# The second product of a gated MLP as seven block products, with its operands and weights in a ring of 512-column tiles

## The chip, the cores and the metric

One core of a Trainium2 chip. The metric is the device time of one execution in microseconds (us), the median of the runs shown. About half a per cent is what a measurement of this kernel can tell from no change.

## The reference, cut to what matters

One inference step of a hybrid decoder layer on 512 prompt tokens and 64 sample tokens (8 sequences of 8): sparse attention, a gated linear recurrence, a merge, and a gated MLP with a causal depthwise convolution of width 3. The change concerns the last lines, the MLP.

```python
def merge_and_ffn(x, o_a, o_b, ma, mb, w_branch, w_out, ffn_norm_g, ffn_w_in, ffn_conv_w, ffn_conv_b, ffn_w_out, conv_buf):
    m = ma * (o_a.astype(x.dtype) @ w_branch[:A_WIDTH]) + mb * (o_b @ w_branch[A_WIDTH:])
    x = x + m @ w_out
    h = rms_norm(x, ffn_norm_g)
    a, b = jnp.split(h @ ffn_w_in, 2, axis=-1)
    ...
    a_conv = ffn_conv_b + sum(a_ext[:, j:j + T] * ffn_conv_w[j] for j in range(FFN_CONV))
    y = x + (jax.nn.silu(a_conv) * b) @ ffn_w_out
```

The model width is 1024 (8 tiles of 128), the hidden width 2816 (22 tiles of 128), and all tensors are fp32.

## The kernel before

Data lie transposed: 128 features on the partitions, the 576 tokens along the free dimension, in two halves of HF = 288 columns. A product in fp32 accuracy is made of three products of a format that TensorE takes at full rate (fp32r): each operand is split into a high part and the rest (`split`, L326: a cast on ScalarE, L330, then a subtraction, L331, on VectorE, or on GpSimd for one split in `pool_every`), and `THREE` multiplies high by high, high by rest and rest by high. `wsplit` (L341) loads a weight tile into `wraw` and splits it into `wsp`; `gemm` (L360) runs, for each contraction tile, the three products on both token halves, 288 columns a matmul.

The kernel runs as one unrolled program in which a scheduler at build time sets each engine's order of instructions; every engine then works through its own queue in that order and waits on semaphores. Stages in order of time: the recurrence, the projections, prompt and sample attention (to about 646 us), `merge` (L1739), `out_proj` (L1783) and `ffn` (L1823). From `merge` on, weights live in the pool `ringF` (L436) with three `wraw` tiles of 1024 columns and three `wsp` tiles of twice 1024, and products in four PSUM tiles `ps_g` of two banks.

`ffn` has two loops. The first (L1834) makes the 22 hidden tiles: for each, one weight tile, 48 matmuls (L1841), an eviction with the norm's factor (L1844 to L1846, VectorE from PSUM), the convolution (L1851 to L1853, VectorE), Silu (L1855 to L1858, ScalarE), a product on GpSimd (L1859), a second weight tile, 48 matmuls (L1861), the gate (L1863) and a split into `g` (L1865), which holds all 22 tiles. The second loop (L1867) makes the 8 output tiles: for each, the residual row `x2r` is loaded (L1869), three weight tiles (8, 8 and 6 blocks, L1874) are multiplied with all of `g`, 132 matmuls into one PSUM tile, one addition on VectorE (L1877) and one store (L1879).

## Time and profile before

| | us |
|---|---|
| median of 3 runs | 1143.64 |
| lowest and highest | 1141.67, 1147.85 |
| the profiled execution, its time | 1141.99 |
| the profiled execution, its span from first to last instruction | 1140.2 |

Times in the rows are those of the profiled execution, counted from its first instruction; 1.8 us of its time lie outside the span. PE is TensorE, PEld its weight loads (which run beside its matmuls), DVE VectorE, ACT ScalarE, POOL GpSimd, SP the queue that issues most DMAs. In a row of groups, `out<-in` names the tiles written and read; behind the first bar stand the busy time and the mean duration of one instruction in ns, behind the second the idle time of that engine just before them and what ended it. A duration includes time that an instruction, once started, is held up.

### The profile page before, as it was taken

Reading aid. Unit: us, or ns where it says so; the run is one execution under the profiler, and the core shown is the slowest. Engines: PE = TensorE matmul, PEld = TensorE weight load, DVE = VectorE, ACT = ScalarE, POOL = GpSimd, SP = SyncE. Lnnn points to the kernel's source line nnn. Section 1 sums busy time; section 2 is a strip of 40 time slices with the busy share of each in tenths; the row PEclk is TensorE's granted clock in tenths of the full one; section 3 lists DMA queues with packets and bytes.
Section 4 is the critical chain, followed back from the end, with each engine's and each line's share of the span. In section 5 each row is a group of like instructions: output and inputs, shape, how many; then the busy total and the mean of one; then the engine's idle time right before and its main releaser. Section 6 shows DMA issues by size and latency. Waiting matters only on the chain.

```text
span 1140.2 us, 21336 instructions
## 1 busy us (share of the span) xinstructions
PE 1092.3 (96%) x7936; PEld 1034.8 (91%) x7936; DVE 658.1 (58%) x1182; ACT 470.8 (41%) x929; POOL 430.4 (38%) x514
## 2 busy tenths in 40 slices
PE   5999999999999899999888799999999999999998
PEld 5997999898999899899665699999999999999998
DVE  6768555674257756887776664665555555511110
ACT  5523443443444567776565643332223222311110
POOL 3654513833374535343365354232223222301010
PEclk8999899999999999999899999999999999999999
DMA  5634456454342422273789675322232223334330
GB/s 199 185 103 155 126 160 194 131 156 149 124 148 59 131 88 72 77 224 101 222 274 284 208 220 183 93 91 88 79 93 75 85 83 93 99 104 124 102 115 21
DMA packets 99273, 151.54 MB, mean 133 GB/s; under 512 B 11233, under 2 KB 66274, under 8 KB 99042
## 3 DMA queue, kind: packets, MB, share of 16 engines
q1 hardware_dynamic: 97714, 146.00, 41.2%
q0 software_dynamic: 1024, 3.54, 1.0%
q8 instruction: 62, 1.02, 0.4%
q10 hardware_dynamic: 432, 0.65, 0.2%
q14 instruction: 41, 0.34, 0.1%
HBM read 131.65 MB, written 22.62 MB: 135 GB/s over the span
## 4 chain that ended last, share of the span: by engine, by line
PE 60%; DVE 6%; ACT 2%; DMA 1%; issue 1%; POOL 1%; SPq 0%; DVEq 0%; ACTq 0%; POOLq 0%
PE ps_g L367 44%; PE ps_g L1200 2%; PE ps_hp L1307 2%; PE ps_sb L1299 2%; PE ps_po L1634 1%; DVE r L1138 1%; PE ps_sa L1267 1%; PE ps_g L1763 1%; PE ps_g L1773 1%; POOL rr L1128 1%; PE ps_sm L1333 1%; PE ps_g L1333 1%; DMA nraw<-in_wk 1%; PE ps_sa L1260 0%; PE ps_sc L1551 0%
## 5 line engine op out<-in xcount | busy, mean ns | idle before, releaser
L367 PE MATMUL ps_g<-h,wsp 128*128 128x288 f32 x2112 | 279.8, 294 | 0.0
L367 PEld LDWEIGHTS ps_g<-h,wsp 128*128 128x128 f32 x2112 | 279.4, 188 | 0.1
L330 ACT CAST wsp<-wraw 128x1024 fp32r<-128x1024 f32 (+3 forms) x142 | 136.3, 966 | 281.0 <-PE ps_g L367 240.5
L367 PE MATMUL ps_g<-xg,wsp 128*128 128x288 f32 x1200 | 182.9, 305 | 16.4 <-ACT wsp L330 8.8
L367 PEld LDWEIGHTS ps_g<-xg,wsp 128*128 128x128 f32 x1200 | 167.7, 193 | 23.6 <-ACT wsp L330 9.0
L331 DVE TENSOR_TENSOR wsp<-wraw,wsp 128x1024 fp32r<-128x1024 f32 (+2 forms) x93 | 113.5, 1222 | 116.4 <-ACT wsp L330 116.1
L331 POOL TENSOR_TENSOR wsp<-wraw,wsp 128x1024 fp32r<-128x1024 f32 (+3 forms) x49 | 108.0, 2203 | 187.1 <-ACT wsp L330 183.7
L367 PE MATMUL ps_g<-g,wsp 128*128 128x288 f32 x1056 | 140.9, 296 | 0.0
L367 PEld LDWEIGHTS ps_g<-g,wsp 128*128 128x128 f32 x1056 | 140.8, 189 | 0.0
L528 PE MATMUL ps_t<-wsp,xg 128*128 128x262 f32 (+1 forms) x480 | 60.9, 285 | 0.0
L528 PEld LDWEIGHTS ps_t<-wsp,xg 128*128 128x128 f32 x480 | 58.9, 189 | 0.1
L903 PE MATMUL ps_pc<-phi,w 128*128 128x256 f32 x256 | 51.0, 290 | 0.0
L330 ACT CAST phi<-praw 128x2048 fp32r<-128x2048 f32 x16 | 30.4, 1901 | 45.7 <-PE ps_pc L903 27.6
L1848 POOL COPY cout<-ext 128x2 f32<-128x2 f32 x22 | 4.1, 184 | 119.0 <-DVE ext L1845 119.0
L1155 POOL TENSOR_TENSOR zg<-zg,rsb 128x576 f32<-128x576 f32 x16 | 27.2, 1699 | 56.4 <-ACT zg L1154 56.4
L1863 DVE TENSOR_TENSOR s<-ps_g,s 128x576 f32<-128x576 f32 x22 | 16.6, 757 | 51.5 <-POOL s L1859 51.5
L1855 ACT ACTIVATE s<-cv 128x512 f32<-128x512 f32 x22 | 13.9, 632 | 78.6 <-DVE cv L1853 78.6
L331 DVE TENSOR_TENSOR plo<-praw,phi 128x2048 fp32r<-128x2048 f32 x14 | 32.7, 2338 | 22.4 <-ACT phi L330 22.2
L903 PEld LDWEIGHTS ps_pc<-phi,w 128*128 128x128 f32 x256 | 42.1, 196 | 0.8 <-issue 0.8
L1274 ACT ACTIVATE sP<-sP,nm 128x128 f32<-128x128 f32 (+3 forms) x64 | 35.6, 560 | 9.2 <-DVE nm L1272 9.2
L1844 DVE TENSOR_TENSOR ext<-ps_g,rs 128x288 f32<-128x288 f32 x22 | 10.1, 457 | 50.8 <-PE ps_g L367 50.7
L1859 POOL TENSOR_TENSOR s<-s,rs 128x576 f32<-128x576 f32 x22 | 31.6, 1434 | 18.8 <-ACT s L1858 18.8
(428 smaller groups left out, 1983.0 us busy)
## 6 DMA issues: line engine op xcount, KB each, us to landing
wraw<-in_wFi SPq DMA_DIRECT2D x44, 512.0 KB
praw<-in_pc SPq DMA_DIRECT2D x256, 64.0 KB
praw<-in_pkv SPq DMA_DIRECT2D x80, 128.0 KB
wraw<-in_wM SPq DMA_DIRECT2D x16, 512.0 KB
wraw<-in_wFo SPq DMA_DIRECT2D x16, 512.0 KB
gbd<-zg SPq DMA_DIRECT2D x24, 288.0 KB
wraw<-in_wBr SPq DMA_DIRECT2D x24, 256.0 KB
pgs<-in_pkv SPq DMA_DIRECT2D x48, 128.0 KB
```

The source lines that it names most:

```text
L330: self.copied = nc.scalar.copy(hi, src)
L331: (eng or nc.vector).tensor_tensor(lo, src, hi.bitcast(F32), op=ALU.subtract)
L367: self.last = nc.tensor.matmul(ps[:, h, 0:HF], w[:, cw, wk, :], (x[cx] if isinstance(x, list) else x[:, cx])[:, xk, h * HF:(h + 1) * HF], ...
L528: nc.tensor.matmul(ps[:, 0:n], self.xg[cx][:, k, j * 128:j * 128 + 128], w[k][:, cw], start=(k == 0 and c == 0), stop=(k == KT - 1 and c = ...
L903: self.nc.tensor.matmul(ps, self.w1[:, cw, j, k], x[cx][:, k], start=start and k == 0 and n == 0, stop=k == 7 and n == 2, skip_group_check ...
L1155: nc.gpsimd.tensor_tensor(z, z, self.rsb, op=ALU.mult)
L1200: self.last = nc.tensor.matmul(ps, w[:, cw, k], self.obs[cx][:, k, c], start=n == 0, stop=n == 11)
L1274: nc.scalar.activation(s[:, b], s[:, b], AF.Exp, scale=-1.0, bias=nm[:, 1 + b, i:i + 1], accum_out=sm[:, 1 + b, i:i + 1])
L1299: nc.tensor.transpose(ps[:, n * 128:n * 128 + 128], sP[i][:, b, j * 128:j * 128 + 128], self.cst("ident"))
L1307: last = nc.tensor.matmul(po[:, i * 128:512], vs[:, j, b].rearrange("p a d -> p (a d)"), pt[:, c, n * 128:(n + m) * 128], start=first, sto ...
L1333: self.last = nc.tensor.matmul(ps, w[:, cw, k], self.oas0[:, cx, k], start=n == 0, stop=n == 11)
L1859: nc.gpsimd.tensor_tensor(s, s, self.rs2, op=ALU.mult)
```

## The change

In `ffn`, the 22 hidden tiles are taken as 11 pairs. For a pair of hidden tiles, a pair of output tiles and the two token halves, the product is one of 2 by 2 blocks, and it is computed with seven block products in place of eight (Winograd's form of Strassen's scheme), each still three matmuls of 288 columns.

- `moving` makes, for each pair of hidden tiles, the seven moving operands: four as they stand or negated, three sums on GpSimd (on VectorE in part for the last pair), all split into high part and rest.
- `down_weights` makes, for a pair of output tiles `q` and a chunk of `m` pairs of hidden tiles, the seven stationary operands: two loads, four sums (three on VectorE, one on GpSimd), seven splits (of the subtractions two on GpSimd).
- The hidden width is taken in chunks of 3, 4 and 4 pairs. After the hidden tile that follows a chunk, `down` runs the chunk's products for the four pairs of output tiles, adds the results to what the earlier chunks left (at first `x2d`) and stores it to a buffer in DRAM, `y2d`; the last chunk stores to `yT`. Within `down`, seven products go to four PSUM banks; two banks receive a second product after the first has been read. The last product of each `q` is issued within the next one. In the last chunk the first four products begin with three of the four pairs.
- From `merge` on, all split weights lie in a ring of ten tiles `w4` of twice 512 columns (before: three `wsp` of twice 1024), and the raw weights in four tiles in place of three. A 1024-column weight tile is split in two halves (`whalves`). The order of the weights in DRAM is changed to match.
- The body of the first loop is moved to a function, `hidden`, and is as before but for the two halves and for the split of its result, which `moving` does for a pair.

```diff
-    a["wFo"] = ktiles(ffn_w_out[0], 128)
+
+    wo = ffn_w_out[0].reshape(NF // 2, 2, 128, 4, 2, 128)
+    a["wFo"] = c(wo.transpose(3, 1, 2, 4, 0, 5)[:, ::-1])
...
+CHUNKS = (3, 4, 4)
+NW4 = 10
...
+    def whalf(self, src, eng=None):
+        sp = self.ring.tile([128, 2, 4, 128], F32R, name="w4", tag="w4", bufs=NW4)[:, :, 0:src.shape[1]]
+        self.split(sp[:, 0], sp[:, 1], src, eng=eng)
+        return sp
...
+    def whalves(self, dram):
+        raw = self.wload(dram, KT, 128)
+        out = []
+        for i in range(2):
+            self.nsplit += 1
+            out.append(self.whalf(raw[:, 4 * i:4 * i + 4], self.nc.gpsimd if self.nsplit % self.pool_every == 0 else self.nc.vector))
+        return out
...
+            self.nraw = 4
...
-        w = self.wsplit(self.a["wO"][d], KT, 128)
+        w = self.whalves(self.a["wO"][d])
...
-                    w = self.wsplit(a["wO"][d], KT, 128)
+                    w = self.whalves(a["wO"][d])
...
+    def moving(self, p, X, Y, last):
+        nc = self.nc
+        e = V if last else G
+        H = lambda y, x: Y[:, y, x * HF:x * HF + HF]
+        ts = p.tile([128, 4, HF], F32, name="ts", tag="ts", bufs=1)
+        flat = Y.rearrange("p a t -> p (a t)")
+        self.split(X[:, 0, 0:2], X[:, 1, 0:2], Y[:, :, 0:HF])
+        G.tensor_tensor(ts[:, 0:2], Y[:, :, HF:T], flat[:, 0:T].rearrange("p (a t) -> p a t", a=2), op=ALU.subtract)
+        e.tensor_tensor(ts[:, 2], ts[:, 0], H(1, 1), op=ALU.subtract)
+        e.tensor_tensor(ts[:, 3], ts[:, 2], H(1, 0), op=ALU.add)
+        self.split(X[:, 0, 3:7], X[:, 1, 3:7], ts)
+        self.split(X[:, 0, 2], X[:, 1, 2], H(1, 1), scale=-1.0)
...
+    def down_weights(self, q, c0, m, early=False):
...
+        fl = lambda t: t[:, :, 0:m]
+        dram = self.a["wFo"][q]
+        raw = []
+        for i in (1, 0):
+            t = self.ring.tile([128, 2, 4, 128], F32, name="wraw", tag="wraw", bufs=self.nraw)
+            nc.sync.dma_start(fl(t), dram[i][:, :, c0:c0 + m])
+            raw.append(fl(t))
+        (a, c), (b, d) = ((t[:, 0], t[:, 1]) for t in raw)
+        s13, s24 = (fl(self.ring.tile([128, 2, 4, 128], F32, name="wsum", tag="wsum", bufs=2)) for _ in range(2))
...
+        w["a"] = self.whalf(a)
+        V.tensor_tensor(s13[:, 0], c, d, op=ALU.add)
+        V.tensor_tensor(s24[:, 0], s13[:, 0], a, op=ALU.add)
+        w["s2"] = self.whalf(s24[:, 0])
+        w["s1"] = self.whalf(s13[:, 0])
+        V.tensor_tensor(s13[:, 1], c, a, op=ALU.add)
+        G.tensor_tensor(s24[:, 1], s24[:, 0], b, op=ALU.add)
+        if early:
+            w["d"] = self.whalf(d)
+        w["s3"] = self.whalf(s13[:, 1])
+        w["b"] = self.whalf(b, G)
+        if not early:
+            w["d"] = self.whalf(d, G)
+        w["s4"] = self.whalf(s24[:, 1])
+        return w
...
+    def down(self, p, n, c0, g, nxt):
...
+        m = len(g)
+        end = c0 + m == NF // 2
...
+        def product(ps, w, x, first, js=range(m)):
+            for j in js:
+                for cw, cx in THREE:
+                    self.last = nc.tensor.matmul(ps, w[:, cw, j], g[j][:, cx, x], start=first and j == 0 and (cw, cx) == (0, 0),
+                                                 stop=j == m - 1 and (cw, cx) == THREE[2], skip_group_check=True)
...
+        def finish(q, w, pc, vv, za, zb, y):
+            product(pc, w["s4"], 2, False)
+            V.tensor_tensor(za[:, HF:T], vv, pc, op=ALU.subtract)
+            for i, z in enumerate((za, zb)):
+                nc.sync.dma_start(self.o["yT"][:, 2 * q + i] if end else self.y2d[n, 2 * q + i], z)
...
+        rest = None
+        A, B, begun = self.bank("g"), self.bank("g"), ()
+        if end:
+            for ps, x, i in ((A[:, 0], "a", 0), (A[:, 1], "s2", 5), (B[:, 0], "s1", 3), (B[:, 1], "d", 6)):
+                product(ps[:, 0:HF], nxt[x], i, True, range(m - 1))
+            begun = (0,)
+        for q in range(4):
+            w = nxt
+            za, zb = (p.tile([128, T], F32, name="z2", tag=t) for t in ("ext", "cv"))
+            src = self.y2d[n - 1] if n else self.x2d
+            nc.sync.dma_start(za, src[2 * q])
+            nc.sync.dma_start(zb, src[2 * q + 1])
+            if q:
+                A, B = self.bank("g"), self.bank("g")
+            pa, pb, pc, pd = (t[:, h, 0:HF] for t in (A, B) for h in range(2))
+            js = range(m - 1, m) if q in begun else range(m)
+            product(pa, w["a"], 0, True, js)
+            t = half("t")
+            nc.scalar.copy(t, pa)
+            product(pb, w["s2"], 5, True, js)
+            vv = half("vv")
+            V.tensor_tensor(vv, t, pb, op=ALU.add)
+            if rest:
+                finish(*rest)
+            product(pc, w["s1"], 3, True, js)
+            product(pb, w["s3"], 4, False)
+            ww = half("ww")
+            V.tensor_tensor(ww, t, pb, op=ALU.add)
+            y = p.tile([128, T], F32, name="y", tag="y", bufs=1)
+            V.tensor_tensor(y[:, HF:T], pc, ww, op=ALU.subtract)
+            product(pa, w["b"], 1, False)
+            V.tensor_tensor(za[:, 0:HF], pa, za[:, 0:HF], op=ALU.add)
+            G.tensor_tensor(vv, za[:, HF:T], vv, op=ALU.add)
+            product(pd, w["d"], 6, True, js)
+            V.tensor_tensor(y[:, 0:HF], pd, ww, op=ALU.subtract)
+            G.tensor_tensor(zb, zb, y, op=ALU.add)
+            if q < 3:
+                nxt = self.down_weights(q + 1, c0, m)
+            rest = (q, w, pc, vv, za, zb, y)
+        finish(*rest)
...
-        g = self.gp.tile([128, 2, NF, T], F32R, name="g")
-                self.split(g[:, 0, i], g[:, 1, i], s)
-                for lo in (0, 8, 16):
-                    n = min(8, NF - lo)
-                    w = self.wsplit(a["wFo"][d][:, lo:lo + n], n, 128)
-                    self.gemm(ps, [(w, range(n), g, range(lo, lo + n))], n0=n0, n=3 * NF)
-                V.tensor_tensor(x2.rearrange("p (a b) -> p a b", a=2), ps[:, :, 0:HF],
...
+            Y, ready, c0 = None, [], 0
+            plan = list(CHUNKS)
...
+                if i % 2 == 0:
+                    Y = p.tile([128, 2, T], F32, name="Y", tag="Y")
+                s = Y[:, i % 2]
+                due = i % 2 == 0 and len(ready) == plan[0]
+                if due or i == NF - 1:
+                    nxt = self.down_weights(0, c0, plan[0], not due)
+                self.hidden(p, i, s, cst, cout, cw, cb)
+                if due:
+                    self.down(p, len(CHUNKS) - len(plan), c0, ready, nxt)
+                    c0 += plan.pop(0)
+                    ready = []
+                if i % 2:
+                    g = self.gp.tile([128, 2, 7, HF], F32R, name="g7", tag="g7", bufs=max(CHUNKS))
+                    self.moving(p, g, Y, i == NF - 1)
+                    ready.append(g)
+            self.down(p, len(CHUNKS) - 1, c0, ready, nxt)
...
```

## Rows read from the trace of the kernel before

**Rows 1.** The page: busy time of the engines; PE's busy tenths in 40 slices.
```profile
PE 1092.3 (96%) x7936; PEld 1034.8 (91%) x7936; DVE 658.1 (58%) x1182; ACT 470.8 (41%) x929; POOL 430.4 (38%) x514
...
PE   5999999999999899999888799999999999999998
```

**Rows 2.** Busy time by stretches; the first line names the columns.
```profile
core 0: us, PE busy (x) PEld busy (x) DVE busy (x) ACT busy (x) POOL busy (x), PEclk, DMA share, GB/s
600.00:620.00 20.00, 17.24 (x113) 12.27 (x114) 14.17 (x36) 11.96 (x24) 11.29 (x11) 1.00 0.90 289
...
649.80:653.20 3.40, 3.40 (x17) 3.40 (x16) 2.93 (x9) 2.52 (x7) 0.00 (x0) 0.50 0.97 331
653.20:660.00 6.80, 6.80 (x53) 6.80 (x53) 3.92 (x7) 2.67 (x5) 3.93 (x4) 1.00 0.81 273
...
722.00:995.00 273.00, 273.00 (x2065) 272.95 (x2064) 161.16 (x204) 81.19 (x133) 77.83 (x120) 1.00 0.28 85
995.00:1136.10 141.10, 141.08 (x1059) 140.84 (x1057) 24.73 (x23) 22.04 (x23) 15.44 (x9) 1.00 0.30 94
1136.10:1140.20 4.10, 0.00 (x0) 0.00 (x0) 0.76 (x1) 0.00 (x0) 0.00 (x0) 1.00 0.19 72
```

**Rows 3.** Waits between engines, 660 us to the end: total, times, longest.
```profile
ACT wsp L330 <- PE ps_g L367: 218.6, 66, 5.5
```

**Rows 4.** Groups of instructions by line and form, 720 us to the end.
```profile
L330 ACT CAST wsp<-wraw 128x1024 fp32r<-128x1024 f32 x57 | 59.9, 1051 | 179.2 <-PE ps_g L367 174.5 <-issue 4.3 <-ACT s L1858 0.4
L331 DVE TENSOR_TENSOR wsp<-wraw,wsp 128x1024 fp32r<-128x1024 f32 x43 | 52.9, 1231 | 86.8 <-ACT wsp L330 86.8
...
L1859 POOL TENSOR_TENSOR s<-s,rs 128x576 f32<-128x576 f32 x22 | 31.6, 1434 | 18.8 <-ACT s L1858 18.8
...
L1853 DVE SCALAR_TENSOR_TENSOR cv<-ext,small,cv 128x592 f32<-128x592 f32 x22 | 18.4, 834 | 0.7
L1863 DVE TENSOR_TENSOR s<-ps_g,s 128x576 f32<-128x576 f32 x22 | 16.6, 757 | 51.5 <-POOL s L1859 51.5
...
L1844 DVE TENSOR_TENSOR ext<-ps_g,rs 128x288 f32<-128x288 f32 x22 | 10.1, 457 | 50.8 <-PE ps_g L367 50.7
```

**Rows 5.** Groups by line and form, whole span: forms of 288, 384 and 512 columns.
```profile
L330 ACT CAST wsp<-wraw 128x512 fp32r<-128x512 f32 x24 | 14.5, 619 | 9.7 <-DMA wraw<-in_wBr 5.1 <-PE ps_g L1200 3.8 <-issue 0.5
...
L1130 DVE TENSOR_TENSOR zn<-zq,rr 128x512 f32<-128x512 f32 x4 | 2.8, 692 | 5.2 <-POOL rr L1128 5.2
...
L1130 DVE TENSOR_TENSOR zn<-zk,rr 128x384 f32<-128x384 f32 x4 | 2.2, 559 | 5.8 <-POOL rr L1128 5.8
...
L331 DVE TENSOR_TENSOR oas<-oa,oas 128x288 fp32r<-128x288 f32 x8 | 3.2, 452 | 1.2 <-ACT oas L330 1.1
...
L1335 POOL TENSOR_TENSOR zm<-zm 128x288 f32<-128x288 f32 x8 | 6.4, 795 | 13.9 <-DVE rr L1599 8.5 <-DVE zm L1334 5.4
```

**Rows 6.** Timeline (start, duration in us): DVE and POOL instructions that meet.
```profile
658.89 1.29 POOL L331 TENSOR_TENSOR wsp<-wraw,wsp 128x512 fp32r<-128x512 f32 x1
...
662.88 1.51 POOL L331 TENSOR_TENSOR wsp<-wraw,wsp 128x512 fp32r<-128x512 f32 x1
...
663.15 0.44 DVE L1764 SCALAR_TENSOR_TENSOR tm<-tm,ps_g 128x288 f32<-128x288 f32 x1
...
767.98 2.39 POOL L331 TENSOR_TENSOR wsp<-wraw,wsp 128x1024 fp32r<-128x1024 f32 x1 [0.80 <-ACT wsp L330]
...
768.71 2.28 DVE L331 TENSOR_TENSOR g<-s,g 128x576 fp32r<-128x576 f32 x1 [0.74 <-ACT g L330]
...
781.77 0.75 DVE L331 TENSOR_TENSOR g<-s,g 128x576 fp32r<-128x576 f32 x1
```

**Rows 7.** Timeline: the first matmul of the merge stage, and the idle time before it.
```profile
649.42 0.40 PE L1773 MATMUL ps_g<-m,wsp 128*128 128x288 f32 x1 [2.65 <-ACT m L333]
```

**Rows 8.** Timeline of the end of the span.
```profile
1136.12 0.76 DVE L1877 TENSOR_TENSOR x2r<-ps_g,x2r 128x576 f32<-128x576 f32 x1 [16.84 <-PE ps_g L367]
1136.90 0.34 SPq L1879 DMA_DIRECT2D out_yT<-x2r  x1
```

More of the change, by code (lines that the diff above doesn't have):

```diff
@@ L336, in wload @@
     def wload(self, dram, kt, cols, queue=None):
-        raw = self.ring.tile([128, kt, cols], F32, name="wraw", tag="wraw")
+        raw = self.ring.tile([128, kt, cols], F32, name="wraw", tag="wraw", bufs=self.nraw)
         self.wdma = (queue or self.nc.sync).dma_start(raw, dram)
@@ L366, in gemm @@
             for h in range(2):
-                self.last = nc.tensor.matmul(ps[:, h, 0:HF], w[:, cw, wk, :], (x[cx] if isinstance(x, list) else x[:, cx])[:, xk, h * HF:(h + 1) * HF],
+                self.last = nc.tensor.matmul(ps[:, h, 0:HF], w[wk // 4][:, cw, wk % 4] if isinstance(w, list) else w[:, cw, wk, :], (x[cx] if isinstance(x, list) else x[:, cx])[:, xk, h * HF:(h + 1) * HF],
                                              start=(n0 + i == 0), stop=(n0 + i == n - 1))
@@ L386, in run @@
             self.x2d = self.dp.tile([KT, 128, T], F32, name="x2d")
+            self.y2d = self.dp.tile([len(CHUNKS), KT, 128, T], F32, name="y2d")
             self.main()
@@ L1772, in out_half @@
         for n, (k, (cw, cx)) in enumerate(todo):
-            self.last = self.nc.tensor.matmul(ps[:, h, 0:HF], w[:, cw, k], self.m[:, cx, k, h * HF:h * HF + HF],
+            self.last = self.nc.tensor.matmul(ps[:, h, 0:HF], w[k // 4][:, cw, k % 4], self.m[:, cx, k, h * HF:h * HF + HF],
                                               start=n == 0, stop=n == len(todo) - 1)
     def begin_out(self, d):
-        w = self.wsplit(self.a["wO"][d], KT, 128)
+        w = self.whalves(self.a["wO"][d])
         ps = self.bank("g")
@@ L1820, in rms2 @@
         nc.vector.reciprocal(self.rs2, self.rs2)
+    def moving(self, p, X, Y, last):
+        nc = self.nc
+        V, G = nc.vector, nc.gpsimd
+        e = V if last else G
[8 more added lines that the diff above has]
+        self.split(X[:, 0, 2], X[:, 1, 2], H(1, 1), scale=-1.0)
@@ new lines, in down @@
+    def down(self, p, n, c0, g, nxt):
+        nc = self.nc
+        V, G = nc.vector, nc.gpsimd
+        m = len(g)
[5 more added lines that the diff above has]
+                                                 stop=j == m - 1 and (cw, cx) == THREE[2], skip_group_check=True)
+        half = lambda name: p.tile([128, HF], F32, name=name, tag=name, bufs=2)
+        def finish(q, w, pc, vv, za, zb, y):
[43 more added lines that the diff above has]
+        finish(*rest)
```

75 lines of the change are left out of this document (36 added, 39 removed).

## The prediction

> **What bounds the kernel now.** I read the page first, then the stretches, then the waits, then the groups. TensorE is busy 96% of the span, and in the slices it stands at 9 tenths from the second half of `merge` (slice 24 of 40) to the last but one [rows 1]. The stretches say it sharper: in the first MLP loop it is busy 273.00 of 273.00 us, in the second 141.08 of 141.10 us, at the full granted clock, while VectorE stands at 59% and 18%, GpSimd at 29% and 11%, and the DMA engines at 0.30 of their time, against 0.90 in an earlier stretch [rows 2]. The waits confirm the direction: the longest total is ScalarE's cast waiting for TensorE to give a weight tile back, 218.6 us in 66 waits [rows 3]. So in the stage that the change rewrites every matmul is on the path, one removed is its whole time saved, and everything else is free until it makes TensorE wait. The question is whether the new work of the other engines does that.
>
> **What is removed.** The second loop has 1056 matmuls (8 output tiles, 22 hidden tiles, 3 products, 2 halves). The change has 4 pairs of output tiles x 11 pairs of hidden tiles x 7 products x 3 = 924, of the same 288 columns and each with its own weight load, as now. One costs 141.08 / 1059 = 133.2 ns [rows 2]; 132 fewer give -17.6 us. This is the only gain, and it cannot be larger than that except through the merge stage.
>
> **What is added on the vector engines.** First the prices. A subtraction or sum of 512 columns takes VectorE 0.69 us, 384 columns 0.56, 288 columns 0.45 [rows 5]; GpSimd 1.29 [rows 6] and 0.80 for 288 [rows 5], so about 1.0 for 384 (an estimate on the line between these two). A ScalarE cast of 512 takes 0.62 [rows 5]. A VectorE reading of PSUM of 288 columns takes 0.46 [rows 4].
>
> Two engines don't simply add up here. VectorE's subtraction into `g` takes 0.75 us alone, but 2.28 when a GpSimd subtraction of 2.39 us had started before it: it ended 0.6 us after that one, so it waited it out [rows 6]. An instruction of VectorE with one operand in PSUM, started inside a GpSimd subtraction, took its usual 0.44 [rows 6]. So I count, as one shared resource, GpSimd's work plus VectorE's instructions with both operands in SBUF, and leave out those that read PSUM.
>
> For one `q` of a chunk of four pairs, TensorE needs 84 x 0.1332 = 11.2 us. VectorE has 5 subtractions and 3 sums, 8 x 0.69 = 5.5; GpSimd 2 subtractions and a sum, 3 x 1.29 = 3.9, and for the results 0.80 + 1.43 [rows 4, 5] = 2.2. The shared resource has 5.5 + 3.9 + 2.2 = 11.6 us of work in 11.2. VectorE's six readings of PSUM, 2.7 us, come on top of its own 5.5: 8.2. ScalarE has 7 casts and a copy, about 4.7. For a chunk of three pairs: TensorE 63 x 0.1332 = 8.4, shared 8 x 0.56 + 3 x 1.0 + 2.2 = 9.7, VectorE 7.2.
>
> A hidden tile (96 matmuls, 12.8 us of TensorE) has, shared: convolution 2 x 0.83 [rows 4], four half weights (two thirds on VectorE) 1.84 + 1.72, the product on GpSimd 1.43 [rows 4], half of a pair's `moving` 1.28 + 1.52, small copies 0.6: 10.0 us. So hidden tiles leave 2.8 us each, and the products of the chunks are over by 0.4 (eight times) and 1.3 us (four times), 8.4 in all if nothing were prepared ahead. But the first set of each chunk is prepared during hidden tiles, and the ring lets a tile be prepared nine products before its use (a slot returns when TensorE has read it), some 11 to 14 us ahead. Inside a chunk only three sets are made: for three pairs 3 x 7.5 + 4 x 2.2 = 31.3 of 33.6 us, for four 3 x 9.4 + 4 x 2.2 = 37.0 of 44.8. That fits, tightly in the first chunk. I take +3 us of TensorE waiting, nearer to 0 (all fits) than to 8.4 (nothing is prepared ahead).
>
> **What is added as waits of TensorE.** The bank `pb` gets its second product (`s3`) only after VectorE has read the first (`s2`). From the second `q` on, two products lie between (2.4 or 3.2 us), against a reading of 0.46: free. In the first `q` of a chunk only `s1` lies between, 1.2 or 1.6 us, in the last chunk 0.4. Behind a two-operand subtraction that is held up by GpSimd (1.29 + 0.69) the reading would be late by about 1.3. Who waits is TensorE, at once. I take 0.5 for each of the three chunks, +1.5 (0 to 5).
>
> The last chunk can't be hidden behind a hidden tile. From the last matmul of hidden tile 21: gate 0.76 [rows 4], sum on GpSimd 1.43, the split of the first two operands 0.75 held up behind that, two sums on VectorE 0.90, a cast of 1152 columns 1.16 and a subtraction of 1.35 (from 1.05 and 1.23 for 1024 [rows 4], an estimate), handoffs: about 6.5 us until the operands of `s2` are there. Cover: 36 begun matmuls and 3 more, 5.2 us. +1.3 us (0 to 3).
>
> The tail: now 4.1 us from the last matmul to the end, of which 0.76 is the addition and 3.3 follow the issue of the store [rows 2, 8]. Then: 0.46, and two stores behind each other instead of one, one issue of 0.34 later, sharing their way. +0.4 us (-0.3 to +1.5).
>
> **What costs nothing, and its cover.** The new traffic (sums read and written again in the first two chunks) brings the first chunk to 768 KB of weights and 1152 KB of rows per `q`, 234 GB/s over 8.4 us, against 289 GB/s carried in an earlier stretch [rows 2]; without that room a late load would add to the +3. On SP a store waits for VectorE, and the loads issued behind it wait too; the four raw tiles are a set ahead. ScalarE has more than half its time free. In `merge` the ring takes 64 KB per partition in place of 36, so later tiles move to other addresses with other former owners; the stage opens with 2.65 us of idle TensorE behind ScalarE [rows 7], so -1.5 to +1.5 there, and I take 0.
>
> **Sum.** -17.6 + 3.0 + 1.5 + 1.3 + 0.4 = -11.4; 1141.99 - 11.4 = 1130.6 us. The sum stands against the profiled execution, which is 1.65 us under the median of the runs shown and inside their range; I leave it there.
>
> **The rivals.** (1) All is hidden: the lead of the ring absorbs the 3 us and the readings are never late. Then -17.6 + 1.3 + 0.4: 1126, down to 1124. For it: ScalarE's idle time, and 37.0 of 44.8 us. Against it: 31.3 of 33.6 in engines that work strictly in order. (2) The shared resource sets the pace and the clock follows. If the 8.4 us are paid and TensorE's gaps reach those that cost clock: after 2.65 us of idle [rows 7] the granted clock stood at 0.50, the 1.2 GHz level, for 3.40 us, in which 17 matmuls ran [rows 2] that take 2.3 us at full clock, so 1.1 us each time. With five such gaps: 1130.6 + 5.4 + 5.5 = 1141.5, no change that can be told. The Trainium skill ("SBUF — State Buffer", Who interferes with whom) has the first half as a rule: a VectorE instruction with two SBUF inputs and a GpSimd instruction that reads SBUF exclude each other, and the later one blocks entirely. By that rule nothing in the 11.6 us can overlap, and the trace agrees (0.75 against 2.28 us). The skill ("TensorE: Matmul & The Clock Gate", HAM oscillation) has the second half: waits of TensorE inside a loop drop its clock again and again; this trace shows it only before the MLP. (3) Slower: VectorE's queue makes both kinds serial. The place is `down`: its PSUM readings stand in order behind subtractions that GpSimd holds up, TensorE waits for each reading, and no preparation runs meanwhile. Then a `q` costs shared plus PSUM work: 11.6 + 2.7 = 14.3 us against 11.2, and 12.4 against 8.4, which is 8 x 3.1 + 4 x 4.0 = 40.8 us more, and 1141.99 - 17.6 + 40.8 + 1.7 = 1167 us. It decides against the change from about 2.1 us lost per `q` (25 us over 12), which would need readings over 2 us later than their slack. Against it: VectorE's own work is 8.2 of 11.2 us. (4) The change doesn't do what it says if TensorE's busy time doesn't fall by 17.6 us, say because the matmuls of one bank in a row run slower; the merge stage's matmuls with one bank, 53 in the 6.8 us after the clock's return [rows 2], speak against it, and I fold it into (2).
>
> **How the numbers follow.** Chances: (1) 0.20, the forecast (1127 to 1138) 0.48, (2) with what ends within half a per cent of the median, 1137.9 to 1149.4, 0.20, (3) and whatever ends above, 0.12. About half a per cent, 5.7 us, is what a measurement of this kernel can tell from no change. Faster by more: 0.68; within: 0.20; slower by more: 0.12. The range takes in (1) with a small gain in merge, and reaches into (2): 1123.5 to 1141.
>
> **What would show it.** Right: 924 matmuls of 288 columns in place of 1056, TensorE busy about 17 us less, its gaps after 722 us summing to 5 to 7 us, lying at the start of chunks and inside the first one, and ended by VectorE's reading (`s3` behind `vv`), by a split, and at the last hidden tile by the split of the moving operands; VectorE's two-operand instructions clearly longer than 0.69 on the mean. Wrong: gaps in every `q` (the shared resource was under-priced, or order in the queues counts more than sums), gaps ended by DMA, a granted clock under 1.00 in the MLP, or a merge stage that moved by more than 1.5 us.

## The result, and the profile after

The change takes 1135.3 us (median of 18 runs) where the kernel before takes 1142.55 us (18 runs): a ratio of 0.9930, 95% interval 0.9915 to 0.9945, so 7 us faster, with 4 us of the forecast gain missing. The profiled execution of the change took 1131.56 us, its span 1129.6 us.

The page of the change, for [rows 1]: TensorE is busy 17.8 us less (1092.3 to 1074.5), and VectorE and GpSimd have over 110 us more each. Of the groups, the block products have 924 matmuls, and in front of them TensorE was idle for 4.1 us.

```profile
PE 1074.5 (95%) x7804; PEld 1015.6 (90%) x7804; DVE 774.5 (69%) x1375; ACT 515.9 (46%) x1064; POOL 547.9 (49%) x613
...
L1903 PE MATMUL ps_g<-g,w 128*128 128x288 f32 x924 | 126.0, 296 | 4.1 <-DVE vv L1936 2.2
```

Busy time by stretches. I cut both kernels at the same three events: the end of the sample's last product, the first matmul on `h` in the MLP, and the last matmul of all. First the kernel before (columns as in [rows 2]):

```profile
646.70:714.90 68.20, 65.55 (x481) 65.48 (x481) 38.26 (x52) 29.93 (x53) 31.96 (x21) 0.97 0.68 217
714.90:1136.10 421.20, 421.18 (x3174) 420.73 (x3172) 188.60 (x230) 106.07 (x159) 95.51 (x133) 1.00 0.29 90
```

Then the change, with the first chunk, the last chunk and the tail set out by themselves:

```profile
643.10:716.70 73.60, 66.47 (x481) 65.73 (x481) 44.43 (x62) 36.11 (x71) 36.47 (x27) 0.95 0.69 220
716.70:1125.70 409.00, 404.92 (x3042) 402.69 (x3040) 297.50 (x413) 146.34 (x279) 214.21 (x227) 1.00 0.36 110
806.00:845.00 39.00, 39.00 (x295) 38.85 (x294) 30.67 (x49) 17.77 (x36) 24.05 (x19) 1.00 0.64 192
1081.30:1125.70 44.40, 41.09 (x301) 39.70 (x299) 28.54 (x42) 12.90 (x23) 21.43 (x16) 1.00 0.25 79
1125.70:1129.60 3.90, 0.01 (x1) 0.00 (x0) 0.46 (x1) 0.00 (x0) 0.00 (x0) 1.00 0.39 151
```

So the MLP is 12.2 us shorter (421.2 to 409.0), the tail 0.2 us shorter (4.1 to 3.9), and the stage ahead, `merge` and `out_proj`, 5.4 us longer with the same 481 matmuls (68.2 to 73.6). That is -7.0 us, which is what the medians say (-7.3). The sample itself ended 3.6 us earlier in this execution of the change, but 0.2 us earlier in a second one (below): that is a difference between executions.

What TensorE waited for in the change, 640 us to the end (total, times, longest):

```profile
PE ps_g L1795 <- ACT m L338: 5.3, 1, 5.3
PE ps_g L1903 <- DVE vv L1936: 2.2, 3, 0.9
PE ps_g L1795 <- DVE m L339: 1.7, 2, 1.4
PE ps_g L1903 <- DVE ww L1942: 1.0, 2, 0.5
...
PE ps_g L1903 <- DVE y L1949: 0.5, 1, 0.5
PE ps_g L1903 <- DVE y L1944: 0.4, 1, 0.4
```

There are two places. One is the opening of the merge (L1795), which answers to [rows 7]: 5.3 us behind ScalarE's `m` instead of 2.65. The other is the block products (L1903): seven waits, 4.1 us, all for readings of PSUM by VectorE; none for a DMA, none for an operand. ScalarE's queue explains the first. This is its timeline at the opening, first of the kernel before, then of the change (start, duration, repeated instructions on one line):

```profile
645.50 1.14 ACT L330 CAST wsp<-wraw 128x512 fp32r<-128x512 f32 x2
646.80 0.77 ACT L1731 COPY oa<-ps_tr 64x32 f32<-64x32 f32 x4 [0.16 <-PE ps_tr L1725]
647.59 1.43 ACT L330 CAST oas<-oa 128x288 fp32r<-128x288 f32 x4
648.93 2.77 ACT L333 ACTIVATE m<-mb 128x288 fp32r<-128x288 f32 x8
```

```profile
643.17 0.77 ACT L1753 COPY oa<-ps_tr 64x32 f32<-64x32 f32 x4 [1.19 <-PE ps_tr L1747]
643.97 1.43 ACT L335 CAST oas<-oa 128x288 fp32r<-128x288 f32 x4
645.30 1.14 ACT L335 CAST w<-wraw 128x512 fp32r<-128x512 f32 x2
646.34 1.66 ACT L335 CAST wsp<-wraw 128x512 fp32r<-128x512 f32 x3
647.90 2.78 ACT L338 ACTIVATE m<-mb 128x288 fp32r<-128x288 f32 x8
```

Before, the weight casts stood ahead of the sample's last copies (`oa`) and `m` came 2.1 us after these began. In the change five weight casts, 2.6 us from start to start, stand between the copies and `m`: 4.7 us. TensorE waits for `m` alone.

### The profile page after: what moved, and what is told of

It is laid out like the page before. It is cut to its first block, busy times and chain, and to the rows that moved or that the text cites. A ratio compares the mean times of both kernels' runs of the same rounds, so it can differ in the third digit from the quotient of the medians.

```text
span 1129.6 us, 21714 instructions
## 1 busy us (share of the span) xinstructions
PE 1074.5 (95%) x7804; PEld 1015.6 (90%) x7804; DVE 774.5 (69%) x1375; ACT 515.9 (46%) x1064; POOL 547.9 (49%) x613
## 3 DMA queue, kind: packets, MB, share of 16 engines
q0 software_dynamic: 1024, 3.54, 1.0%
## 5 line engine op out<-in xcount | busy, mean ns | idle before, releaser
L387 PE MATMUL ps_g<-h,w 128*128 128x288 f32 x2112 | 281.0, 294 | 0.0
L387 PEld LDWEIGHTS ps_g<-h,w 128*128 128x128 f32 x2112 | 279.8, 188 | 0.1
L387 PE MATMUL ps_g<-xg,wsp 128*128 128x288 f32 x1200 | 185.5, 308 | 15.6 <-ACT wsp L335 8.8
L387 PEld LDWEIGHTS ps_g<-xg,wsp 128*128 128x128 f32 x1200 | 170.2, 196 | 22.0 <-ACT wsp L335 9.0
L335 ACT CAST w<-wraw 128x512 fp32r<-128x512 f32 (+1 forms) x140 | 84.8, 611 | 149.7 <-PE ps_g L387 103.9
L1903 PE MATMUL ps_g<-g,w 128*128 128x288 f32 x924 | 126.0, 296 | 4.1 <-DVE vv L1936 2.2
L1903 PEld LDWEIGHTS ps_g<-g,w 128*128 128x128 f32 x924 | 123.2, 188 | 5.9 <-DVE vv L1936 2.9
L336 POOL TENSOR_TENSOR w<-wraw,w 128x512 fp32r<-128x512 f32 (+1 forms) x58 | 79.5, 1374 | 61.2 <-ACT w L335 57.7
L336 DVE TENSOR_TENSOR w<-wraw,w 128x512 fp32r<-128x512 f32 (+1 forms) x82 | 74.7, 913 | 16.5 <-ACT w L335 11.8
L335 ACT CAST wsp<-wraw 128x1024 fp32r<-128x1024 f32 (+2 forms) x66 | 57.9, 895 | 41.4 <-PE ps_g L387 21.6
L336 POOL TENSOR_TENSOR wsp<-wraw,wsp 128x1024 fp32r<-128x1024 f32 (+2 forms) x23 | 47.7, 2077 | 55.5 <-ACT wsp L335 52.0
L336 DVE TENSOR_TENSOR wsp<-wraw,wsp 128x1024 fp32r<-128x1024 f32 (+2 forms) x43 | 55.7, 1297 | 23.6 <-ACT wsp L335 23.2
```

The lines of the kernel that those rows point to most:

```text
L335: self.copied = nc.scalar.copy(hi, src)
L336: (eng or nc.vector).tensor_tensor(lo, src, hi.bitcast(F32), op=ALU.subtract)
L387: self.last = nc.tensor.matmul(ps[:, h, 0:HF], w[wk // 4][:, cw, wk % 4] if isinstance(w, list) else w[:, cw, wk, :], (x[cx] if isinstance ...
L1903: self.last = nc.tensor.matmul(ps, w[:, cw, j], g[j][:, cx, x], start=first and j == 0 and (cw, cx) == (0, 0), stop=j == m - 1 and (cw, cx ...
```

## Experiments

All times in us, each from one profiled execution but the ratio, which is of all runs to the runs of the kernel before on the same chip. "Ahead" is the stretch from the sample's last product to the first matmul on `h`; "idle" is TensorE's idle time within the MLP.

| kernel | ratio, 95% interval | opening gap | ahead | MLP | idle |
|---|---|---|---|---|---|
| before | 1 | 2.65 | 68.2 | 421.2 | 0.0 |
| the change | 0.9930, 0.9915 to 0.9945 | 5.26 | 73.6 | 409.0 | 4.1 |
| the change again | 0.9924, 0.9900 to 0.9948 | 5.25 | 73.6 | 409.0 | 4.2 |
| its MLP alone | 0.9904, 0.9873 to 0.9935 | 2.65 | 69.8 | 411.2 | 4.2 |
| its addresses alone | 1.0032, 1.0012 to 1.0052 | 6.20 | 71.9 | 421.2 | 0.0 |
| its half tiles alone | 1.0016, 0.9995 to 1.0037 | 2.66 | 68.4 | 421.2 | 0.0 |
| three raw tiles | 0.9944, 0.9923 to 0.9965 | 3.69 | 71.6 | 411.0 | 5.3 |
| ScalarE's order | 0.9925, 0.9898 to 0.9952 | 3.69 | 74.6 | 408.5 | 3.7 |
| ring of eight | 1.0110, 1.0080 to 1.0141 | 4.21 | 70.7 | 436.2 | 20.4 |
| no early beginning | 0.9928, 0.9903 to 0.9954 | 5.25 | 73.8 | 408.2 | 3.6 |
| six products | 0.9854, 0.9796 to 0.9912 | 5.25 | 73.2 | 399.7 | 9.6 |
| no GpSimd in the weights | 0.9905, 0.9875 to 0.9936 | 5.25 | 74.0 | 405.9 | 1.7 |
| six, no GpSimd | 0.9794, 0.9766 to 0.9822 | 5.25 | 74.2 | 391.8 | 3.9 |
| MLP alone and no GpSimd | 0.9885, 0.9854 to 0.9915 | 2.65 | 68.2 | 407.3 | 1.1 |

### The change again

No edit.

> The change itself, unchanged, to be timed beside the other kernels on the same chip: 0.9915 to 0.9945 of the kernel before, as in its own measurement. Its second profile shows what is the same in every execution: an opening gap of 5.25 us ahead of the merge, MLP gaps of 3.6 to 4.3 us with the two of 0.93 us in the last chunk.

The opening gap, the stage ahead, the MLP and its two gaps of 0.93 and 0.92 us came out the same to 0.1 us: both losses belong to the program and not to one execution. Inside the stage ahead the parts shifted: the granted clock stood at 0.50 for 10.2 us behind the opening gap, where the first profile has 6.9, and the later gaps sum to 1.4 us, where it has 1.9.

### Where the 5.4 us ahead of the MLP come from

First the MLP's edit without the merge's: whole tiles and the old ring up to `out_proj`, the new ring only behind it.

```
-        with self.banks("psF", g=(2, 4)), self.pool("ringF", 3) as self.ring:
+        ringF = self.pool("ringF", 3)
+        with self.banks("psF", g=(2, 4)):
+            self.ring = ringF.__enter__()
...
-            with self.pool("fp", side="right") as self.fp:
+            with self.pool("fp", side="right") as self.fp, self.pool("ringM", 3, "right") as ringM:
                 self.out_proj()
                 mp.__exit__(None, None, None)
+                ringF.__exit__(None, None, None)
+                self.ring, self.nraw = ringM, 4
...
-        w = self.whalves(self.a["wO"][d])
+        w = self.wsplit(self.a["wO"][d], KT, 128)
```

> The changed MLP with the merge and the output projection as they were before (whole weight tiles, the old 36 KB ring; the ring of ten tiles is opened only for the MLP, on the other side of SBUF). In the profile of the change the MLP is 12.2 us shorter (421.2 to 409.0 us) while the stretch from the last product of the sample to the first of the MLP is 5.4 us longer (68.2 to 73.6 us). Theory: the two are independent, and the loss comes from the edit of the merge alone (the ring opened early), so that here the stretch ahead of the MLP is back at 68 +/- 1 us and the whole comes to 0.989 to 0.9915 of the kernel before (1130 to 1133 us against 1142.5). Rival: the loss is one of the run or goes with the MLP (its other instructions move the plan of everything ahead of it), so that this kernel is no faster than the change as it stands, 0.992 to 0.995.

The opening gap is 2.65 us again and the stage ahead 69.8, 0.8 beyond the bound but 3.8 less than in the change: most of the loss is the merge's own, and the MLP's gain stands by itself. What is left above the kernel before is mostly clock: behind the same gap of 2.65 us the granted clock stood at 0.50 for 6.8 us here and for 3.4 us there, and TensorE's busy time in the stage is 66.9 us against 65.5. The whole came to 1131.6 us; its ratio can't be told from the change's, so that it is the stretches that show the effect. (Its MLP is 2.2 us longer than the change's with the same idle time; see the last section.)

Then the kernel before with one part of the edit at a time. Its addresses:

```
+            pad = self.pool("pad")
+            pad.__enter__().tile([128, 7168], F32, name="pad")
             self.mp = mp.__enter__()
...
```

> The kernel before with 28 KB left empty between its ring and the merged tile, so that m and the merge's tiles lie at the addresses that they have in the change; nothing else differs. Theory A (addresses: the tiles of the merge lie over others of the sample, that come free later): the loss of the change ahead of the MLP appears here, +3 to +5.4 us, 1.003 to 1.005. Theory B (what matters is in which order ScalarE takes the weight casts and the operand m, and that is set by the size of the ring's tiles and their number): in this kernel's program one cast of a 512-column weight tile stands between the sample's outputs and m, where the change has five, so +0.6 us at most, 0.999 to 1.001.

Theory A holds and B's bound was wrong. An empty 28 KB between the ring and the merged tile, and nothing else, makes the stage 3.8 us longer (68.2 to 71.9) and the kernel slower, 1.0032. In ScalarE's queue three weight casts, not one, now stand between the copies `oa` and `m`, where the kernel before has none. By the start-to-start times (5.67 us from the copies to `m` against 2.13) they are some 1.6 of the 3.5 us, and the wait for `mb` is the other 1.9:

```profile
646.69 1.14 ACT L330 CAST wsp<-wraw 128x512 fp32r<-128x512 f32 x2
649.07 0.61 ACT L330 CAST wsp<-wraw 128x512 fp32r<-128x512 f32 x1
651.57 0.78 ACT L333 ACTIVATE m<-mb 128x288 fp32r<-128x288 f32 x2 [1.89 <-DMA mb<-gbd]
```

SyncE's queue shows why `mb` is late. Before (first fence) the two loads of `mb` stand in the queue from 638.26 and are both issued by 645.68; with the pad (second fence) both stand behind a weight load that was not issued until 645.51, and `m` began at 651.57, when the first of them had come, in place of 648.93.

```profile
637.29 0.86 SPq L338 DMA_DIRECT2D wraw<-in_wBr  x2
638.26 7.42 SPq L1748 DMA_DIRECT2D mb<-gbd  x2
```

```profile
645.51 0.33 SPq L338 DMA_DIRECT2D wraw<-in_wBr  x1
646.32 0.97 SPq L1751 DMA_DIRECT2D mb<-gbd  x2
```

So tiles that move change the order in which the scheduler puts the queues, and half of the loss appears in another queue than in the change. Its half tiles, in `out_proj` and in both loops of the MLP (six half tiles in the room of the three whole ones):

```
-        w = self.wsplit(self.a["wO"][d], KT, 128)
+        w = self.whalves(self.a["wO"][d])
...
```

> The kernel before with each of its whole weight tiles in the output projection and the MLP split in two halves of 512 columns (six half tiles in the room of three whole ones, the engine of the subtraction chosen for each half), its second product as it was. Theory C (two casts and two subtractions for a tile in place of one cost the merge its time): +3 to +5.4 us ahead of the MLP, and in the MLP nothing, 1.003 to 1.005. Theory B (ScalarE's order): in this program the casts of the first output weight stand ahead of the sample's last outputs as in the kernel before, so the stretch ahead of the MLP stays at 68 +/- 1 us and the whole within 0.998 to 1.002.

Theory C falls: 68.4 us ahead, and an interval that holds 1. Twice as many casts and subtractions, at half the size, cost the stage nothing that can be told. The fourth raw tile:

```
-            self.nraw = 4
+            self.nraw = 3
```

> The change with three raw weight tiles in place of four; ring, halves and MLP stay as changed. Theory B (ScalarE's order): in this program the first output weight's casts stand ahead of the sample's last outputs again, and nothing but the sample's outputs ahead of m, so the opening gap of the merge is back near 2.65 us, the half-clock stretch behind it near 3.4 us, and the loss of 5.4 us ahead of the MLP falls to 0 to 1.5. If the MLP needs no fourth raw tile the whole comes to 0.989 to 0.9915. Rival: the fourth raw tile is what keeps the MLP's weights ahead (its raw tiles arrive two at a time), and with three TensorE waits for casts behind a DMA there: the MLP 2 to 6 us longer than 409.0, and the whole 0.992 to 0.997.

Between the two: ScalarE's order was the old one but for two casts, the gap 3.69, the stage 71.6, so 2 of the 5.4 us. And the rival has its share too: 1.2 us more idle time in the MLP, with a gap of 0.93 us in the first chunk (it ends with a reading of `vv`, not with a DMA). The whole is no better than the change. Last, the order of ScalarE alone, at the addresses of the change:

```
+            ready = self.scaled
             self.begin_out(0)
...
-                with self.tc.issue_after(self.keyed_last.ins) if MKL else nullcontext():
+                with self.tc.issue_after((ready if d < 3 else self.keyed_last).ins):
```

(`self.scaled` is the last scaling that `split` issued.)

> The change with the three casts of the branch's weights, which stand ahead of the eight scalings of m in ScalarE's queue, put behind them; ring, addresses and MLP as in the change. Three casts take 0.52 us each from start to start. Theory (the opening gap is ScalarE's queue, not a wait for memory): the gap falls from 5.25 us by 1.6 to 3.6 +/- 0.3 us, and the stretch ahead of the MLP from 73.6 to 70 to 72. Rival (the scalings wait for their data or for their place): the gap stays at 5 us or more.

The first half came out: without the three casts the gap is 3.69 us, 1.56 less, so for these 1.6 of the 2.6 us it was ScalarE's queue that TensorE waited for, and not memory. The second half did not: the stage took 74.6 us. Its waits, from the sample's end to the MLP:

```profile
PE ps_g L1796 <- ACT m L338: 3.7, 1, 3.7
PE ps_g L1796 <- DVE m L339: 2.5, 2, 1.7
```

and a second stretch at half the clock behind them (columns as above):

```profile
673.80:677.20 3.40, 3.40 (x16) 3.40 (x16) 3.40 (x6) 2.08 (x5) 2.58 (x3) 0.51 0.94 320
```

In sum the stage's gaps are 1.0 us less than in the change (6.2 against 7.1) and TensorE's busy time is 2.0 us more (68.4 against 66.5), the second stretch at half the clock among it. The three casts were needed for the matmuls on `oas`, which in the change follow the first matmul on `m`; with the casts behind `m` these are not ready, and TensorE waits 0.8 us for VectorE's half of `m` instead. The other 1.7 us lie where the change has 1.4 and 0.3.

What is shown is that opening the ring later takes the loss away (69.8 us, and 68.2 in the last kernel below), and that in the kernel before 28 KB of other addresses cost 3.8 us by themselves. That the addresses do it in the change too, and not the number of tiles in the ring, is not shown: there the opening loss shows in ScalarE's queue alone, and with one raw tile less 2 of the 5.4 us go. Why the scheduler orders the queues so was not settled.

### What the MLP's 4.1 us of idle time are

The longest two gaps of the MLP, 0.93 us at 1087.28 and 0.92 at 1090.08, end with the reading of `vv`. VectorE and GpSimd ahead of the first one, in the change:

```profile
1083.71 0.69 DVE L336 TENSOR_TENSOR w<-wsum,w 128x512 fp32r<-128x512 f32 x1
1084.43 1.66 DVE L1876 TENSOR_TENSOR wsum<-wraw 128x512 f32<-128x512 f32 x1
1086.01 1.78 DVE L1880 TENSOR_TENSOR wsum<-wraw 128x512 f32<-128x512 f32 x1
1087.72 0.44 DVE L1936 TENSOR_TENSOR vv<-t,ps_g 128x288 f32<-128x288 f32 x1
```

```profile
1084.05 1.49 POOL L336 TENSOR_TENSOR w<-wraw,w 128x512 fp32r<-128x512 f32 x1 [4.75 <-ACT w L335]
1085.90 1.35 POOL L336 TENSOR_TENSOR w<-wraw,w 128x512 fp32r<-128x512 f32 x1 [0.36 <-ACT w L335]
```

Each of VectorE's two sums ended 0.55 us after GpSimd's subtraction, whenever it had started. To see whether that is the cause, GpSimd's three operations of a quarter go to VectorE:

```
-        G.tensor_tensor(s24[:, 1], s24[:, 0], b, op=ALU.add)
+        V.tensor_tensor(s24[:, 1], s24[:, 0], b, op=ALU.add)
...
-        w["b"] = self.whalf(b, G)
+        w["b"] = self.whalf(b)
-            w["d"] = self.whalf(d, G)
+            w["d"] = self.whalf(d)
```

> The change with the three operations that GpSimd has in each quarter's weights (the subtractions of b and d and the second sum of s24) given to VectorE; nothing else is changed. In the change's profile the two longest gaps of TensorE in the MLP, 0.93 and 0.92 us at 1087 and 1090 us, end with VectorE's reading of vv, which stands behind sums of the weights that took 1.66 and 1.78 us while GpSimd ran subtractions of 1.49 and 1.35 us; the same sum takes 0.68 us where GpSimd is idle. Theory (VectorE is held while GpSimd reads two operands from SBUF): VectorE's sums fall to 0.7 us, the three operations cost it 3 x 0.69 us for a quarter but free it of more, and the two gaps shrink to under 0.3 us each: the MLP 0 to 2 us shorter than 409.0. Rival (what makes VectorE late is the number of instructions in its queue): 2.1 us more of them for each quarter, so the gaps grow to 1.5 us or more and others open in every quarter, +3 to +15 us.

The theory holds, and the gain is more than forecast: the MLP is 3.1 us shorter, 2.4 of it idle time, though VectorE has 36 instructions more. The same place in VectorE's timeline:

```profile
1086.52 0.69 DVE L1876 TENSOR_TENSOR wsum<-wraw 128x512 f32<-128x512 f32 x1
1087.12 0.69 DVE L1880 TENSOR_TENSOR wsum<-wraw 128x512 f32<-128x512 f32 x1
1087.72 0.45 DVE L1936 TENSOR_TENSOR vv<-t,ps_g 128x288 f32<-128x288 f32 x1
```

Both sums take 0.69 us again, the first gap is gone and the second is 0.53 us (over the bound of 0.3). VectorE's busy time over the MLP rose by 6 us only (297.5 to 303.5) where the 36 operations alone are worth some 23 (24 of 512 columns by 0.69, 12 of 384 by 0.56): the rest must have been waiting that counts as busy. GpSimd's fell from 214.2 to 166.2 us.

Two of the seven waits are of another kind and stay: 0.55 us for `ww` and 0.55 for `y`, both in the last `q`. VectorE was idle ahead of these readings in the change, so nothing held them:

```profile
1119.35 0.45 DVE L1942 TENSOR_TENSOR ww<-t,ps_g 128x288 f32<-128x288 f32 x1 [1.14 <-PE ps_g L1903]
1123.34 0.46 DVE L1949 TENSOR_TENSOR y<-ps_g,ww 128x288 f32<-128x288 f32 x1 [1.13 <-PE ps_g L1903]
```

The matmuls behind them are the last 36 of the program, and TensorE has no others to run meanwhile. The kernel without GpSimd in the weights has the same two, 0.55 us each.

### What the ring and the early beginning are for

```
-NW4 = 10
+NW4 = 8
```

> The change with eight half tiles in its ring instead of ten: a quarter's seven and one ahead, where the change has three ahead. In the change's profile the first chunk, where VectorE and GpSimd together have the most to do, shows no gap on TensorE, against the 3 us that were forecast for it. Theory: the ring's lead is what absorbed it. Then here gaps on TensorE appear in the first chunk (0.5 to 3 us) and the MLP is 2 to 6 us longer than the 409.0 us of the change. Rival: the scheduler's spread of the work is enough, and the lead is idle: 409 +/- 1 us.

The MLP is 27 us longer, far above the forecast, and the kernel slower than before; but the gaps are not where the theory has them. TensorE's costliest wait in this MLP:

```profile
PE ps_g L387 <- ACT w L335: 8.1, 9, 2.3
```

It lies not in the products but in the hidden tiles (L387), whose weights come out of the same ring. Whatever ended them, the waits at L387 sum to 13.0 of the 20.4 us, and every one stands in the last 16 us ahead of a chunk (5.2, 4.7 and 3.1 us), while the first seven weight tiles of the chunk are being made: beside seven there is room for one. Inside the first chunk one gap of 0.20 us is left. The longest of the nine in this line, 2.3 us, ended with a cast at 801.09 that stood in ScalarE's queue behind an operand of the products, which waited for GpSimd's sums:

```profile
800.03 1.15 ACT L335 CAST g<-ts 128x1152 fp32r<-128x1152 f32 x1 [3.49 <-POOL ts L1856]
801.09 0.61 ACT L335 CAST w<-wraw 128x512 fp32r<-128x512 f32 x1
```

The granted clock fell to 0.50 in four places in the MLP, as in this one at the end of the first hidden tiles, with 23 matmuls in 6.8 us:

```profile
802.20:809.00 6.80, 5.68 (x23) 4.97 (x21) 1.54 (x4) 0.56 (x1) 0.00 (x0) 0.50 0.32 104
```

The other 10.9 of the 27 us are busy time, mostly matmuls at half the clock. So the ring's length is what lets a chunk's operands be made beside a hidden tile. That it absorbs the load inside the first chunk is not shown: TensorE's stops ahead of the chunk gave the other engines time as well. The early beginning does not do the like:

```
-        if end:
+        if end and False:
```

> The change without the early beginning of the last chunk's first quarter: the 36 matmuls on the first three pairs run where the others do, behind the last pair's operands. The change's profile has no gap at that place, against the 1.3 us that were forecast. Theory: the 36 matmuls (4.8 us) are what covers the last pair's sums, cast and subtraction; without them a gap of 4 to 6.5 us opens ahead of the last chunk, while the two gaps of 0.93 us behind it go, since each product has twelve matmuls again for VectorE's reading: +2.5 to +5 us against the change. Rival: the operands were ready anyhow, and the order makes no difference: 0 +/- 1 us.

The rival holds. The ratio is that of the change, the MLP 0.8 us shorter. TensorE's timeline at the end of the last hidden tile and after it:

```profile
1079.46 5.72 PE L1903 MATMUL ps_g<-g,w 128*128 128x288 f32 x42
1085.53 5.92 PE L1903 MATMUL ps_g<-g,w 128*128 128x288 f32 x42 [0.34 <-ACT g L335]
1093.10 1.07 PE L1903 MATMUL ps_g<-g,w 128*128 128x288 f32 x6 [1.65 <-DVE vv L1936]
```

Without being told, the scheduler put 42 matmuls of the products ahead of the operand that was late, and only 0.34 us were lost there (the 1.65 behind it is again a reading of `vv`); what the source writes out by hand was there anyway.

### How near the next bound is

```
-            product(pc, w["s4"], 2, False)
```

> The change with one of the seven block products left out (the fourth weight sum by the third operand); its weight tile is still loaded, summed, split, and every reading of PSUM stays. It leaves 132 of the 924 matmuls out, so part of the output is not computed. Theory: TensorE is the bound in the MLP and a matmul is worth its full start-to-start time, 132.3 to 133.3 ns; so -17.5 us against the change (1118 us), less what more waiting takes: VectorE and GpSimd have the same work in 12% less time, +1 to +4, that is 1119 to 1122, 0.979 to 0.982 of the kernel before. Rival: after the seventh part VectorE or GpSimd is already the bound of the chunks, and a matmul less is worth little: -5 us or less, 1130 us.

Between the two. This kernel leaves the `s4` products out. The 132 matmuls gave 9.3 us in the MLP (409.0 to 399.7) and 9.0 in the medians (against the change again, on the same chip), of 17.5: idle time rose by 5.5 us, and the clock fell once, at 953.7, for 3.4 us with 16 matmuls. TensorE now waits first for `Y` itself, the end of a hidden tile on VectorE:

```profile
PE ps_g L1903 <- DVE Y L2016: 4.8, 2, 2.5
```

The same with the three operations on VectorE (the edit above):

> The kernel with one block product left out, now also without GpSimd in the weights of the products. With six products and GpSimd as in the change, the 132 matmuls less (17.5 us) gave only 9.3 us in the MLP, the gaps grew from 4.1 to 9.6 us and the clock fell to half for one stretch of 3.4 us. Theory (VectorE held by GpSimd is what takes the rest): the gaps are back under 4 us, no half clock in the MLP, and the MLP takes 387 to 392 us against 399.7. Rival (VectorE's own work is the bound, whatever GpSimd does): the gaps stay at 8 us or more, the MLP at 397 us or more.

The theory holds, at the edge of its numbers: idle time 3.9 us, no half clock in the MLP, 391.8 us. Against seven products without GpSimd (405.9) the same 132 matmuls are now worth 14.1 us. So more than half of what was lost (4.8 of 8.2 us) goes with GpSimd's work in the weights, and 3.4 of the 17.5 us are still lost to something else.

### Both repairs

The MLP's edit alone, with the weights on VectorE: the two diffs above.

> The two edits that each helped, together: the merge and the output projection as in the kernel before with the ring of ten tiles opened for the MLP alone, and none of GpSimd in the weights of the block products. If their causes are independent, the opening gap is 2.65 us, the gaps of TensorE in the MLP sum to under 2 us, the last product of the sample to the last of the program takes 478 us (482.6 in the change, 489.3 in the kernel before), and the whole is 0.984 to 0.989 of the kernel before, about 1127 us. Rival (what is left is the same stall seen from two sides): no better than either edit alone, 0.990.

1128.5 us, 0.9885: 0.4 points under the change measured on the same chip in the same session (0.9924), though the intervals overlap by a little. From the sample's end to the last matmul it takes 475.5 us, 2.5 less than expected. The waits of TensorE that the profile names from there on are the opening gap of old and two readings in the last quarter:

```profile
PE ps_g L1798 <- ACT m L338: 2.7, 1, 2.7
PE ps_g L1906 <- DVE y L1952: 0.6, 1, 0.6
PE ps_g L1906 <- DVE ww L1945: 0.5, 1, 0.5
```

Each repair took its own gaps away, so the two losses have separate causes. The stage ahead is 1.6 us shorter than with the MLP's edit alone, mostly because the stretch at half the clock was 3.4 us long and not 6.8; the merge is the same in both, so that part is not the edit's.

## Why the prediction was right, and where it was not

The forecast was 1130.6 us, 11.4 under the execution before; the medians say 7.3, inside the range. That the profiled execution, 1131.56 us, lies within 1 us of the forecast is luck: its sample ended 3.6 us earlier. The sum itself has errors of opposite sign: 0.4 us too much for the MLP and 0.6 for the tail, 5.4 too little for the merge. The mechanism was the right one: TensorE bounds the MLP, and fewer matmuls shorten it by their time less what VectorE and GpSimd make it wait. Step by step:

- **-17.6 for the matmuls.** TensorE's busy time fell by 17.8 us over the span and by 16.3 in the MLP. Most of the 1.3 us between 17.6 and 16.3 goes with the waits: a matmul takes 296 ns from start to end and 133 from start to start, and ahead of a wait nothing runs beside the last one, 7 x 0.16 = 1.1 us (an estimate from these rows). Rival (4) falls.
- **+3.0 in the first chunk.** It was 0: TensorE is busy 39.00 of 39.00 us there, in both profiles of the change (the MLP's edit alone has one gap of 0.82 us). The chunk's own sum, 31.3 of 33.6 us, said that it fits, and the 3 us were taken on top of it, between 0 and 8.4, with no row that sizes them. Whether the sum was right or the ring's lead did more than it allowed stays open, since the ring of eight lost its time elsewhere.
- **+1.5 for the readings of `pb`.** The cause was named rightly, a reading that stands behind a sum that GpSimd holds up, and so was its delay ("about 1.3", against two sums 1.0 and 1.1 us too long). It was 2.2 us: 0.93 and 0.92 at the start of the last chunk, and 0.3 in the second chunk behind two sums of 0.69 us, which nothing held. The forecast had it in every chunk alike, and called it free from the second `q` on; but the second gap of the last chunk ends with the `vv` of the second `q` (the chunk's second reading of that line), whose first products the scheduler had pulled forward. The other readings, `ww` and `y`, were put at nothing and cost 1.9. The diff shows why they can: three banks, not two, receive a second product (`b`, `s3` and `s4`), and the sum has a wait for one. The Trainium skill ("SBUF — State Buffer", Who interferes with whom) says that a VectorE instruction with two inputs in SBUF contends with a GpSimd instruction that reads SBUF. The profiles agree: 1.66 and 1.78 us with GpSimd at work, 0.69 and 0.69 without.
- **+1.3 for the last chunk's beginning.** It was 0. The operands did come late (the cast ended 5.9 us after the last matmul on `h`), but I counted only the matmuls that the source begins early, 39 with those behind them; the scheduler finds more, 81 in a row from 1076.39 us on. (Of the seven moving operands that are made there, three stand as they are or negated and four are sums, by three instructions; the forecast's prices are those of the three.)
- **+0.4 for the tail.** It was -0.2, inside its bounds.
- **0 for the merge, -1.5 to +1.5.** This is the step that failed: +5.4, and a merge stage that moves by more than 1.5 us is one of the prediction's own signs of being wrong. The text saw that later tiles would get other addresses, and took it for worth nothing on balance. Of the 5.4, 2.6 are in the opening gap, 1.9 in three gaps later in the stage, and 0.9 in matmuls at half the clock (busy time 65.55 to 66.47 for the same 481). The addresses alone cost 3.8 us in the kernel before; half tiles cost nothing that can be told.

So the waits of the MLP were put at 5.8 and the MLP's gain at 11.8; they were 4.1 and 12.2. The signs of being right came only in part: the gaps sum to 4.1 us and not to 5 to 7, and none lies in the first chunk. The sum missed by the stage that the change was not meant for. Rival (1), all hidden, was right for the first chunk and the last hidden tile. Rival (2) did not occur: the granted clock is 1.00 throughout the MLP; with a ring of eight or six products it falls there. Rival (3) did not occur.

## What to carry to other kernels

When a pool grows, price the stages that share its memory, whether or not their code changes: 28 KB of nothing cost 3.8 us here, because tiles at other addresses made the scheduler put the queues in another order; open the larger pool where it is first needed. When TensorE is the bound and VectorE reads PSUM for it, look at what GpSimd runs at that moment: giving VectorE more work, and GpSimd less, made VectorE's readings earlier. And a forecast of waits needs the room in the ring as much as the load of the engines: with three tiles beside a set of seven TensorE never waited for a weight, with one the MLP was 27 us longer.

## What the runs showed of the hardware that was not expected

TensorE, never idle and at full clock, runs the same matmuls of 288 columns at two paces. Stretches of 80 us in the MLP, of the kernel before and of the change (the change again has x608, the last kernel above x602):

```profile
1000.00:1080.00 80.00, 80.00 (x602) 80.00 (x601) 14.46 (x14) 13.83 (x14) 7.36 (x4) 1.00 0.37 113
```

```profile
1000.00:1080.00 80.00, 80.00 (x607) 80.00 (x607) 60.52 (x80) 27.22 (x54) 43.01 (x47) 1.00 0.31 95
```

From start to start that is 133.3 against 132.2 ns in the mean. The slow pace is a row of 140, 131, 131 and 132 ns over and over; the fast one goes between 130 and 136. It belongs to the program and the stretch, not to the execution (607 and 608), and not to the loop either: the MLP of the kernel before has the fast one in its first loop and the slow one in its second [rows 2], the kernels with the ring on the other side have the slow one in nearly the whole MLP. On 3040 matmuls the difference is up to 3 us, and so the last kernel's MLP (407.3 us, 406.2 of them busy) is longer than that of the change without GpSimd in the weights (405.9, 404.1 busy), with less idle time. What sets the pace was not tried.
